# The down projection of a feed-forward block: seven block products in another order, on two chains of banks in turns, with the first unit's operands in one shared piece of SBUF

## The chip, the cores and the metric

The kernel runs on one core of one Trainium2 chip. The metric is device time in microseconds (us): the median of several executions. One more execution was recorded by the hardware profiler. TensorE multiplies matrices and writes PSUM, VectorE (DVE) and ScalarE (ACT) do element-wise work, GpSimd (POOL) does too but not on PSUM, and SyncE (SP) issues the transfers (DMA). Each engine works through its own instructions in the order in which the program lists them.

## The reference

Two layers on 1024 rows of width 1024. Each layer runs a mixer, a feed-forward block and an embedding gate:

```python
D_FF = 2816
def swiglu(h, w_gate, w_up, w_down):
    return (jax.nn.silu(h @ w_gate) * (h @ w_up)) @ w_down
...
        h = h + swiglu(rmsnorm(h, norm_ffn_g[i]), ffn_w_gate[i], ffn_w_up[i], ffn_w_down[i])
        e = rmsnorm(p[i] @ ple_w_proj[i], ple_post_norm_g[i])
        h = h + e * jax.nn.sigmoid(rmsnorm(h, ple_norm_g[i]) @ ple_w_gate[i])
```

What is changed is the last product of `swiglu`, a [1024 x 2816] by [2816 x 1024] matrix product (called "down" below, once in each layer), and the last line, the embedding gate (`ple`).

## The kernel before

**How a product is kept exact.** Operands are split in a high part that TensorE takes as fp32r and a low part that is the rest. A product is three matmuls: high by high, high by low, low by high. ACT makes the high part (a cast), DVE the low part (a subtraction).

**The seven block products.** The product is cut in 2 x 2 blocks and done with seven block products in place of eight. The left factor's seven combinations are made in the gate/up stage before (`ffn_gu`) and written to device memory (`gfD`): three of them as they are, four as sums that POOL makes in `wino` (`Sg`). The right factor has eight: four blocks of the weights as loaded (`wr_dn`, index 0 to 3) and four sums that POOL makes (`T_dn`, index 4 to 7). A line of `steps` (L965) names: the left combination, the right one, the chain of banks (a or b), whether the banks start anew, and the quarter of the result `h` (row parity, column half) to which the banks are read out after this step. Chain a starts once in a unit and chain b twice. A chain that does not start anew goes on adding to what its banks hold, after they have been read out.

**Units and steps.** The 11 pairs of weight rows go in units of 2, 3, 3 and 3 pairs (L967). A unit runs the seven steps, so there are 28 steps in a down stage. A step multiplies, for each of four row pieces (`tp`), the unit's 2 or 3 pairs with three matmuls each: 24 matmuls in the first unit, 36 in the others, 924 in a down stage. After each row piece its bank is read out into `h`, by ACT the first time that a quarter is written (L1025) and by DVE with an addition afterwards (L1023).

**What a step needs first.** The left operand is loaded into a slot (L1004); ACT casts it (`y`, L1009), DVE subtracts (`x`, L1010); ACT and DVE split the right operand into `wh` and `wl` (L1012, in the helper L108 and L109). A slot holds x, y, wh and wl for up to three pairs (24 KB of each partition). There are four such slots, s0, s1, s2 and the one of `mk(7)`, which the steps take in turn, and one special place for step 3 of the first unit. A slot is free again when the matmuls of its step are done. In the first unit a slot of 24 KB holds 16 KB of operands.

**Order of the work.** The order of each engine's instructions is fixed when the program is built: a planner simulates the run with a cost model and takes, at each engine, the ready instruction that comes first in the program's order. `high_priority` moves a piece to an earlier place in that order; `after` (`issue_after`) only puts instructions behind a named one on the same engine. Pools that follow one another share memory, so a tile of the down stage waits until the tiles of the gate/up stage under it are done with.

**After the last unit.** `ple` normalises each of the eight row tiles (`norm`, L1115: ACT squares, POOL takes the root, DVE scales, TensorE transposes into PSUM, ACT and DVE split), even tiles first, and then runs two halves of gate products (`gate`, L1118) with weights that `weights` (L1102) casts on ACT and subtracts on POOL (L1110, L1111). The norms of the even tiles are placed just before the last step of the last unit (`self.even`, L995). At most two scaled rows (`hn`) exist at a time.

Of the kernel before, what the change touches and what calls it, by code (L numbers as in the profile page):

```python
# [9 lines left out]
F32 = mybir.dt.float32  # L10
F32R = mybir.dt.float32r
# [4 lines left out]
ALU = mybir.AluOpType  # L16
# [4 lines left out]
P = 128  # L21
# [42 lines left out]
class _K:  # L64
# [879 lines left out]
    def ffn_down(self, es, l, gD):  # L944
        nc, A = self.nc, self.A
        v, gp = nc.vector, nc.gpsimd
        h = self.h
        self.psum(es, f"ffpd{l}", a=4, b=4)
        mk = lambda i: self.pool(es, f"ffn{l}d{i}")
        if l:  # L950
            rw, ta, tb, s0 = mk(2), mk(1), mk(5), mk(0)
        else:
            s0, ta, rw, tb = mk(0), mk(1), mk(2), mk(5)
        s1 = mk(3)
        s2 = mk(4)
        self.pad(es, 1, f"ffp2{l}")
        tc_ = mk(6)
        sp = [s0, s1, s2, mk(7)]
        self.pad(es, 2, f"ffp3{l}")
        s3 = mk(8)  # L960
        slots = itertools.chain(sp[:3], itertools.cycle((s0, s1, sp[3], s2)))
        raws = itertools.cycle(((self.W, "wr", 2), (self.W, "wr", 2), (rw, "dr", 3), (rw, "dr", 3), (rw, "dr", 3)))
        sums = itertools.cycle(((tc_, "T", 2), (tc_, "T", 2), (ta, "T", 1), (tb, "T", 1)))

        steps = ((0, 0, "a", True, (0, 0)), (1, 2, "b", True, (0, 0)), (3, 4, "b", True, (1, 1)), (4, 5, "a", False, (0, 1)),  # L965
                 (6, 3, "b", False, (0, 1)), (5, 6, "a", False, (1, 1)), (2, 7, "a", False, (1, 0)))
        units = ((0, 1), (2, 3, 4), (5, 6, 7), (8, 9, 10))  # L967
        seen = set()
        rest = iter(range(NT))
        raw_of = {}  # L970

        def load(p):
            home, tag, bufs = next(raws)
            raw_of[p] = home.tile([P, 2048], F32, tag=tag, bufs=bufs, name=f"wr_dn{l}_{p}")
            nc.sync.dma_start(raw_of[p], A[f"w_dn{l}"][p])

        for p in units[0]:
            load(p)
        for ui, pairs in enumerate(units):
            m = len(pairs)  # L980
            ws = []
            for p in pairs:
                raw = raw_of.pop(p)
                q = raw.rearrange("p (q n) -> p q n", q=4)
                home, tag, bufs = next(sums)
                T = home.tile([P, 4, 512], F32, tag=tag, bufs=bufs, name=f"T_dn{l}_{p}")
                self.wino(gp, [T[:, i] for i in range(4)], [q[:, i] for i in range(4)], "right")
                ws.append([q[:, i] for i in range(4)] + [T[:, i] for i in range(4)])
            banks = {}
            if not ui:  # L990
                for tp in range(4):
                    banks["b", tp] = self.tp(f"pdb{l}_0_1_{tp}", "b")
            for si, (gi, wi, chain, first, (hr, hc)) in enumerate(steps):
                if si == len(steps) - 1:
                    self.even = self.tc.cur_priority  # L995
                nm = f"{l}_{ui}_{si}"
                if (ui, si) == (0, 3):
                    x, y = [self.np.tile([P, D], F32R, tag="hn", bufs=2, name=f"sl{f}{nm}").rearrange("p (j n) -> p j n", j=2) for f in "xy"]
                    slot = s3.tile([P, 2, 2, 512], F32R, name=f"slw{nm}")
                    wh, wl = slot[:, 0], slot[:, 1]  # L1000
                else:
                    slot = next(slots).tile([P, 4, 3, 512], F32R, tag="slot", bufs=1, name=f"sl{nm}")
                    x, y, wh, wl = [slot[:, i, :m] for i in range(4)]
                nc.sync.dma_start(x.bitcast(F32), gD[pairs[0]:pairs[-1] + 1, :, gi, :].rearrange("j p n -> p j n"))  # L1004
                if si == 3 and ui + 1 < len(units):
                    for p in units[ui + 1]:
                        load(p)
                with self.after([self.last_sum] if ui == 0 and si else None):
                    nc.scalar.copy(y, x.bitcast(F32))  # L1009
                    v.tensor_tensor(x, x.bitcast(F32), y.bitcast(F32), op=ALU.subtract)  # L1010
                    for i in range(m):
                        self.split(wh[:, i], wl[:, i], ws[i][wi])  # L1012
                for tp in range(4):
                    if first and (ui or chain == "a"):
                        banks[chain, tp] = self.tp(f"pd{chain}{nm}_{tp}", chain)
                    ps = banks[chain, tp]
                    c = slice(tp * P, (tp + 1) * P)
                    for i in range(m):
                        for k, (a, b) in enumerate(((y, wh), (y, wl), (x, wh))):
                            nc.tensor.matmul(ps, a[:, i, c], b[:, i, :], start=first and i == 0 and k == 0, stop=i == m - 1 and k == 2, skip_group_check=True)  # L1020
                    hv = h[:, 2 * tp + hr, hc * 512:(hc + 1) * 512]
                    if (hr, hc) in seen:
                        v.tensor_tensor(hv, ps, hv, op=ALU.add)  # L1023
                    else:
                        nc.scalar.copy(hv, ps)  # L1025
                seen.add((hr, hc))
                t = next(rest, None) if 7 * ui + si in range(9, 25, 2) else None
                if t is not None:
                    x = self.np.tile([P, D], F32, tag="hn", bufs=2, name=f"hres{l}_{t}")
                    nc.sync.dma_start(x, self.hB[t * P:(t + 1) * P, :])  # L1030
                    gp.tensor_tensor(h[:, t, :], h[:, t, :], x, op=ALU.add)
# [50 lines left out]
    def ple(self, l, out):  # L1082
        nc, A = self.nc, self.A
        v, gp = nc.vector, nc.gpsimd
        h = self.h
        order = (0, 2, 4, 6, 1, 3, 5, 7)
        with ExitStack() as es:
            mk = lambda nm: self.pool(es, f"ple{l}{nm}")
            x = lambda nm: mk(nm).tile([P, KC, 512], F32R, name=f"{nm}_p{l}")
# [3 lines left out]
            hT = [hh, hl]  # L1093
            w1 = [mk("w1a"), mk("w1b")]
            fp = mk("e")
            self.pad(es, 9, f"plp0{l}")
            w0 = mk("w0")
            gB = self.bcast_row(self.np2, A[f"g_pn{l}"], D, "gB", f"gB_pn{l}")
            self.psum(es, f"plps{l}", tp=8)
            self.ttags = itertools.cycle(["tp"])  # L1100

            def weights(u):  # L1102
                w = []
                for kh in range(2):
                    raw = self.W.tile([P, 2048], F32, tag="wr", bufs=2, name=f"wr_pg{l}_{u}{kh}")
                    nc.sync.dma_start(raw, A[f"w_pg{l}"][u, kh])
                    wt = [(w1[kh] if u else w0).tile([P, 4, 512], F32R, name=f"w{f}_pg{l}_{u}{kh}") for f in "hl"]
                    for i in range(0, 4, 2):
                        r = raw.rearrange("p (k n) -> p k n", k=4)[:, i:i + 2]
                        nc.scalar.copy(wt[0][:, i:i + 2], r)  # L1110
                        gp.tensor_tensor(wt[1][:, i:i + 2], r, wt[0][:, i:i + 2].bitcast(F32), op=ALU.subtract)  # L1111
                    w.append(wt)
                return w

            def norm(t):  # L1115
                self.norm_T(self.np2, h[:, t, :], gB, hT, t, f"p{l}", hnp=self.np)

            def gate(u, t, w):  # L1118
                cs = slice(u * 512, (u + 1) * 512)
# [14 lines left out]
                nc.sync.dma_start(out[rows, cs], h[:, t, cs])  # L1134

            w = weights(0)
            with self.tc.high_priority(self.tc.cur_priority - self.even):
                for t in order[:4]:
                    norm(t)
            for t in order[:4]:  # L1140
                gate(0, t, w)
                norm(t + 1)
            for t in order[4:]:
                gate(0, t, w)
            w = weights(1)
            for t in order:
                gate(1, t, w)
        self.dump(f"h_ple{l}", h)
# [605 lines left out]
```

## Time and profile before

| | us |
|---|---|
| median of 3 runs (2988.99 to 2994.79) | 2994.49 |
| profiled execution, its own time | 2983.25 |
| its span, first to last instruction | 2981.5 |
| TensorE busy in the span | 2868.9 (96%) |
| DVE busy | 1871.5 (63%) |
| ACT busy | 1256.5 (42%) |
| POOL busy | 1062.8 (36%) |
| down stage of layer 0, first matmul to first transpose of the gate | 1126.53 to 1355.58 |
| down stage of layer 1 | 2652.43 to 2878.28 |

TensorE is busy nearly all the time, so what can be gained without fewer matmuls lies in the stretches in which it stands still or runs at a lower granted clock. A row of a timeline gives the start, the duration, the engine, the line, the operation, output and input by the program's names, and how many like it follow one another. In brackets stands how long the engine was idle just before, and which instruction ended that. Matmuls overlap, so a matmul's own duration (some 390 ns) is longer than the distance from one to the next.

### The profile page before, as it was taken

The numbers are of one execution on the slowest core, as the hardware profiler recorded it, in microseconds if no ns is written. First come the engines' busy times: TensorE is split into PE (matmuls) and PEld (weight loads), VectorE is DVE, ScalarE is ACT, GpSimd is POOL, SyncE is SP. The second block draws the span as 40 slices with busy tenths as digits, with TensorE's granted clock in tenths as the row PEclk, the third lists the DMA queues.
The fourth block names the chain that finished last, engine by engine and source line by source line (L and its number), as shares of the span: only waits on it lengthen the run. The fifth ranks groups of instructions, "written<-read, shape, count | busy, mean of one in ns | idle before, by whom it ended". The sixth has DMA issues, their size and how long they took to land.

```text
span 2981.5 us, 47762 instructions
## 1 busy us (share of the span) xinstructions
PE 2868.9 (96%) x19211; PEld 2387.9 (80%) x19211; DVE 1871.5 (63%) x3274; ACT 1256.5 (42%) x2226; POOL 1062.8 (36%) x931
## 2 busy tenths in 40 slices
PE   7999998999999998999999999999999999999999
PEld 7989876797888886887887777788677888877877
DVE  5799995555444448984466767664455444469871
ACT  4467725554333334334445455443233333334341
POOL 1341000114444436434213443342144444566342
PEclk9999998999999998999999999999999999999999
DMA  4122165201323225534242232223711322255422
GB/s 145 50 51 93 57 191 205 92 22 39 113 102 106 106 103 204 195 112 130 106 132 91 94 114 94 90 90 113 263 64 71 113 106 103 98 190 183 157 90 92
DMA packets 119822, 340.80 MB, mean 114 GB/s; under 512 B 11696, under 2 KB 34608, under 8 KB 101936
## 3 DMA queue, kind: packets, MB, share of 16 engines
q1 hardware_dynamic: 119600, 337.74, 32.9%
q8 instruction: 151, 2.47, 0.3%
q14 instruction: 71, 0.58, 0.1%
HBM read 240.64 MB, written 97.06 MB: 113 GB/s over the span
## 4 chain that ended last, share of the span: by engine, by line
PE 78%; DVE 10%; POOL 3%; DMA 3%; ACT 3%; issue 2%; SPq 0%; DVEq 0%; ACTq 0%; POOLq 0%
PE pga L852 16%; PE pgb L852 8%; PE pso L1361 7%; PE psp L1130 6%; PE pda L1020 6%; PE pdb L1020 4%; PE psz L216 4%; PE pgc L852 4%; PE psow L237 3%; PE psz L1621 2%; PE pskqv L227 2%; POOL T_dn L780 2%; PE y L743 2%; DVE sc L467 1%; PE pswob L237 1%
## 5 line engine op out<-in xcount | busy, mean ns | idle before, releaser
L1020 PE MATMUL pda<-sl 128*128 128x512 f32 x1008 | 236.5, 393 | 15.2 <-DVE h L1023 14.2
L1020 PEld LDWEIGHTS pda<-sl 128*128 128x128 f32 x1008 | 190.2, 189 | 57.4 <-ACT sl L108 15.5
L782 POOL TENSOR_TENSOR S<-wr_gu 128x512 f32<-128x512 f32 x44 | 67.0, 1523 | 399.9 <-DMA wr_gu<-in_w_gu_dram 392.4
L1020 PE MATMUL pdb<-sl 128*128 128x512 f32 x792 | 188.4, 395 | 3.9 <-DVE h L1023 2.5
L1020 PEld LDWEIGHTS pdb<-sl 128*128 128x128 f32 x792 | 151.0, 191 | 38.1 <-DVE h L1023 4.5
L109 DVE TENSOR_TENSOR w2l_gu<-S,w2h_gu 128x1024 fp32r<-128x1024 f32 x44 | 69.3, 1575 | 164.7 <-ACT w2h_gu L108 164.6
L1361 PE MATMUL pso<-hh,wl_od 128*128 128x512 f32 x384 | 157.1, 409 | 0.0
L1361 PE MATMUL pso<-hh,wh_od 128*128 128x512 f32 x384 | 156.9, 408 | 0.0
L1361 PE MATMUL pso<-hl,wh_od 128*128 128x512 f32 x384 | 156.5, 408 | 0.0
L1009 ACT CAST sl<-sl 128x1536 fp32r<-128x1536 f32 (+1 forms) x54 | 74.9, 1387 | 140.5 <-DMA sl<-gfD 140.5
L108 ACT CAST w2h_gu<-S 128x1024 fp32r<-128x1024 f32 x44 | 46.3, 1052 | 186.4 <-PE pga L852 94.1
L780 POOL TENSOR_TENSOR T_dn<-wr_dn 128x512 f32<-128x512 f32 x44 | 82.8, 1908 | 115.9 <-DVE sl L109 61.1
L1379 DVE SCALAR_TENSOR_TENSOR c<-pso,odcw,c 128x509 f32<-128x509 f32 (+1 forms) x144 | 107.1, 744 | 25.9 <-ACT c L1376 24.3
L1010 DVE TENSOR_TENSOR sl<-sl 128x1536 fp32r<-128x1536 f32 (+1 forms) x54 | 103.5, 1919 | 30.9 <-ACT sl L1009 30.8
L227 PE MATMUL pskqv<-wh_kqv,hh 128*128 128x256 f32 x384 | 109.4, 285 | 0.3 <-ACT wh_kqv L108 0.3
L227 PE MATMUL pskqv<-wh_kqv,hl 128*128 128x256 f32 x384 | 108.7, 283 | 0.0
L227 PE MATMUL pskqv<-wl_kqv,hh 128*128 128x256 f32 x384 | 108.3, 283 | 0.0
L603 DVE TENSOR_SCALAR_CACHE_REDUCE tk_junk<-sc,tk_f 128x1024 int8<-128x1024 f32 (+5 forms) x111 | 102.6, 924 | 1.8
L1130 PE MATMUL psp<-wh_pg,hh_p 128*128 128x512 f32 x256 | 100.5, 393 | 0.0
L153 POOL TENSOR_SCALAR nss_f<-nss_f 128x1 f32<-128x1 f32 x16 | 3.2, 198 | 272.5 <-ACT junk_f L152 272.5
L1130 PE MATMUL psp<-wh_pg,hl_p 128*128 128x512 f32 x256 | 99.7, 390 | 0.0
L1130 PE MATMUL psp<-wl_pg,hh_p 128*128 128x512 f32 x256 | 99.7, 389 | 0.0
(543 smaller groups left out, 9017.0 us busy)
## 6 DMA issues: line engine op xcount, KB each, us to landing
wr_gu<-in_w_gu_dram SPq DMA_DIRECT2D x44, 1024.0 KB
sl<-gfD SPq DMA_DIRECT2D x42, 768.0 KB
gfD<-Sg SPq DMA_DIRECT2D x22, 1024.0 KB
wr_dn<-in_w_dn_dram SPq DMA_DIRECT2D x22, 1024.0 KB
wr_od<-in_w_qkv_dram SPq DMA_DIRECT2D x12, 1024.0 KB
cD<-c SPq DMA_DIRECT2D x24, 512.0 KB
gfD<-g SPq DMA_DIRECT2D x22, 512.0 KB
wr_z<-in_w_z_dram SPq DMA_DIRECT2D x10, 1024.0 KB
```

The costliest lines, as they stand in the source:

```text
L216: nc.tensor.matmul(ps[:M, f * 512:(f + 1) * 512], a[:, kc, c], b[f][:, kc, :], start=(kc == 0 and i == 0), stop=(kc == KC - 1 and i == 2))
L227: nc.tensor.matmul(out, a[:, kc, c], b[:, kc, :], start=(kc == 0 and i == 0), stop=(kc == KC - 1 and i == 2))
L237: nc.tensor.matmul(ps[:, f * 512:(f + 1) * 512], a[:, kc, tsl], b[:, f * 512:(f + 1) * 512], start=(kc == 0 and i == 0), stop=(kc == nk - ...
L603: v.tensor_scalar(jk[:, :n], sc[b], fb, 0.0, op0=op, op1=ALU.add, accum_out=c)
L780: sub = lambda o, x, y: eng.tensor_tensor(o, x, y, op=ALU.subtract)
L852: nc.tensor.matmul(bank, a[:, kc, :], b[:, kc, :], start=first and kc == 0 and m == 0, stop=kc == 3 and m == 2, skip_group_check=True)
L1009: nc.scalar.copy(y, x.bitcast(F32))
L1010: v.tensor_tensor(x, x.bitcast(F32), y.bitcast(F32), op=ALU.subtract)
L1020: nc.tensor.matmul(ps, a[:, i, c], b[:, i, :], start=first and i == 0 and k == 0, stop=i == m - 1 and k == 2, skip_group_check=True)
L1130: nc.tensor.matmul(ps, a[:, kc, c], b, start=kc == 0 and i == 0, stop=kc == KC - 1 and i == 2)
L1361: nc.tensor.matmul(ps[:, f * 512:(f + 1) * 512], a[:, kc, :], b[f][:, kc, :], start=(kc == 0 and i == 0), stop=(kc == KC - 1 and i == 2))
L1379: nc.vector.scalar_tensor_tensor(c[:, e:(f + 1) * 512], ps[:, e - d:(f + 1) * 512 - d], cw[:, k:k + 1], c[:, e:(f + 1) * 512], op0=ALU.mul ...
```

## The change

Four things are changed, all in `ffn_down` and `ple`:

- The order of the steps: (4, 5) comes before (3, 4) and (5, 6) before (6, 3), so that the chains run a b a b a b a in place of a b b a b a a. In units 1 and 3 the two chains change places, so that a unit begins on the chain that the unit before did not end on.
- The slots: s1 and s2 become one tile `sl12` of 48 KB. The first unit takes three thirds of it (16 KB each, offsets 0, 2, 4), the later units two halves (0 and 3). With s0, `mk(7)` and the special place, the first unit's steps 0 to 4 have five places that none of them shares. In the last unit `mk(7)` is not used, so three slots go round.
- The homes of the raw weights and of the sums of the last unit: pair 10 is loaded into the `dr` buffers in place of the `wr` ones; pairs 9 and 10 take `ta` and `tb`.
- `ple`: its first weights lie 8 KB further up (pad 17 for 9), and the casts of its second weights come behind the last early norm on ACT.

```diff
-        s1 = mk(3)
-        s2 = mk(4)
+        s12 = mk(3).tile([P, 6 * 2048], F32R, name=f"sl12_{l}")
...
-        sp = [s0, s1, s2, mk(7)]
+        s7 = mk(7)
...
-        slots = itertools.chain(sp[:3], itertools.cycle((s0, s1, sp[3], s2)))
-        raws = itertools.cycle(((self.W, "wr", 2), (self.W, "wr", 2), (rw, "dr", 3), (rw, "dr", 3), (rw, "dr", 3)))
-        sums = itertools.cycle(((tc_, "T", 2), (tc_, "T", 2), (ta, "T", 1), (tb, "T", 1)))
-
-        steps = ((0, 0, "a", True, (0, 0)), (1, 2, "b", True, (0, 0)), (3, 4, "b", True, (1, 1)), (4, 5, "a", False, (0, 1)),
-                 (6, 3, "b", False, (0, 1)), (5, 6, "a", False, (1, 1)), (2, 7, "a", False, (1, 0)))
+
+        slots = itertools.chain((s0, 0, 2, None, 4, s0, 0), (s7, 3, s0, 0) * 3 + (s7, 3), (s0, 0, 3, s0, 0, 3, 0))
+        ra, rb = (self.W, "wr", 2), (rw, "dr", 3)
+        raws = iter((ra, ra, rb, rb, rb, ra, ra, rb, rb, rb, rb))
+        sums = itertools.chain(((tc_, "T", 2), (tc_, "T", 2), (ta, "T", 1), (tb, "T", 1)) * 2, ((tc_, "T", 2), (ta, "T", 1), (tb, "T", 1)))
+
+        steps = ((0, 0, "a", True, (0, 0)), (1, 2, "b", True, (0, 0)), (4, 5, "a", False, (0, 1)), (3, 4, "b", True, (1, 1)),
+                 (5, 6, "a", False, (1, 1)), (6, 3, "b", False, (0, 1)), (2, 7, "a", False, (1, 0)))
...
-                if (ui, si) == (0, 3):
+                chain = "ab"[(chain == "b") ^ (ui % 2)]
+                slot = next(slots)
+                if slot is None:
...
-                    slot = next(slots).tile([P, 4, 3, 512], F32R, tag="slot", bufs=1, name=f"sl{nm}")
-                    x, y, wh, wl = [slot[:, i, :m] for i in range(4)]
+                    if isinstance(slot, int):
+                        slot = s12[:, slot * 2048:][:, :m * 2048]
+                    else:
+                        slot = slot.tile([P, 6144], F32R, tag="slot", bufs=1, name=f"sl{nm}")[:, :m * 2048]
+                    slot = slot.rearrange("p (i j n) -> p i j n", i=4, j=m)
+                    x, y, wh, wl = [slot[:, i] for i in range(4)]
...
-            self.pad(es, 9, f"plp0{l}")
+            self.pad(es, 17, f"plp0{l}")
...
-            def weights(u):
+            def weights(u, marks=None):
...
+                    with self.after(marks):
+                        for i in range(0, 4, 2):
...
             for t in order[:4]:
                 gate(0, t, w)
-                norm(t + 1)
+                marks = norm(t + 1)
             for t in order[4:]:
                 gate(0, t, w)
-            w = weights(1)
+            w = weights(1, marks[:1])
```

## Rows read from the trace of the kernel before

**Rows 1.** Stretches of layer 0's down stage: busy us (and instructions) of each engine
```profile
1126.00:1187.00 61.00, 50.07 (x191) 38.87 (x190) 52.37 (x46) 25.81 (x42) 46.36 (x27) 0.86 0.51 185
1187.00:1323.00 136.00, 135.09 (x596) 111.32 (x595) 120.82 (x135) 53.09 (x69) 57.99 (x27) 1.00 0.50 168
```
**Rows 2.** Timeline of TensorE in layer 0's down stage
```profile
1126.53 5.65 PE L1020 MATMUL pda<-sl 128*128 128x512 f32 x24
...
1137.71 1.66 PE L1020 MATMUL pdb<-sl 128*128 128x512 f32 x6 [1.46 <-DVE g L937]
...
1142.67 0.79 PE L1020 MATMUL pda<-slw,sly 128*128 128x512 f32 x1 [3.06 <-DVE slw L109]
...
1175.48 2.90 PE L1020 MATMUL pda<-sl 128*128 128x512 f32 x6 [5.73 <-DVE h L1023]
...
1232.87 16.60 PE L1020 MATMUL pda<-sl 128*128 128x512 f32 x72 [0.91 <-DVE h L1023]
...
1339.26 16.48 PE L1020 MATMUL pda<-sl 128*128 128x512 f32 x72
1355.58 1.91 PE L193 MATMUL tp_p<-cf,hn_p 128*128 128x128 f32 x16
```
**Rows 3.** Timeline of TensorE in layer 1's down stage and behind it
```profile
2652.43 1.09 PE L1020 MATMUL pda<-sl 128*128 128x512 f32 x4
...
2697.93 2.90 PE L1020 MATMUL pda<-sl 128*128 128x512 f32 x6 [6.42 <-DVE h L1023]
...
2755.26 12.52 PE L1020 MATMUL pda<-sl 128*128 128x512 f32 x54 [0.90 <-DVE h L1023]
...
2878.28 1.91 PE L193 MATMUL tp_p<-cf,hn_p 128*128 128x128 f32 x16
...
2884.51 1.09 PE L193 MATMUL tp_p<-cf,hn_p 128*128 128x128 f32 x8 [2.66 <-DVE hn_p L203]
```
**Rows 4.** Short stretches; the third number from the right is the granted clock
```profile
1147.00:1151.50 4.50, 4.50 (x11) 3.44 (x11) 4.50 (x6) 0.59 (x1) 4.50 (x4) 0.50 0.91 337
...
2666.00:2669.00 3.00, 1.76 (x6) 0.81 (x6) 3.00 (x2) 1.10 (x2) 3.00 (x3) 1.00 0.03 13
```
**Rows 5.** Timeline of DVE in layer 0, before the longest wait
```profile
1157.62 1.64 DVE L1010 TENSOR_TENSOR sl<-sl 128x1024 fp32r<-128x1024 f32 x1 [3.10 <-ACT sl L1009]
1159.18 1.88 DVE L109 TENSOR_TENSOR sl<-wr_dn,sl 128x512 fp32r<-128x512 f32 x3
1162.60 1.29 DVE L109 TENSOR_TENSOR sl<-T_dn,sl 128x512 fp32r<-128x512 f32 x2 [1.54 <-ACT sl L108]
...
1165.55 4.61 DVE L1010 TENSOR_TENSOR sl<-sl 128x1536 fp32r<-128x1536 f32 x2 [0.46 <-ACT sl L1009]
...
1171.28 3.45 DVE L109 TENSOR_TENSOR sl<-wr_dn,sl 128x512 fp32r<-128x512 f32 x2
1174.66 0.68 DVE L1023 TENSOR_TENSOR h<-pda,h 128x512 f32<-128x512 f32 x1
```
**Rows 6.** Queue of SP: issues of the left operands, in both layers
```profile
1139.78 0.41 SPq L1004 DMA_DIRECT2D sl<-gfD  x1
...
2845.83 0.36 SPq L1004 DMA_DIRECT2D sl<-gfD  x1
```
**Rows 7.** Timeline of POOL in layer 0: the last sum of the last group
```profile
1155.64 1.28 POOL L780 TENSOR_TENSOR Sg<-g,Sg 128x512 f32<-128x512 f32 x1
```
**Rows 8.** Timeline of DVE in layer 1: opening, last unit, gate
```profile
2679.55 1.65 DVE L1010 TENSOR_TENSOR sl<-sl 128x1024 fp32r<-128x1024 f32 x1 [1.82 <-ACT sl L1009]
...
2697.11 0.68 DVE L1023 TENSOR_TENSOR h<-pda,h 128x512 f32<-128x512 f32 x1
...
2851.71 1.75 DVE L1010 TENSOR_TENSOR sl<-sl 128x1536 fp32r<-128x1536 f32 x1
...
2881.81 2.64 DVE L203 SCALAR_TENSOR_TENSOR hn_p<-h,ss_p,gB_pn 128x1024 f32<-128x1024 f32 x1
```
**Rows 9.** Timeline of ACT in layer 1's last unit: a cast behind its load
```profile
2850.10 1.48 ACT L1009 CAST sl<-sl 128x1536 fp32r<-128x1536 f32 x1 [2.59 <-DMA sl<-gfD]
```

More of the change, by code (lines that the diff above doesn't have):

```diff
@@ L1107, in weights @@
                     wt = [(w1[kh] if u else w0).tile([P, 4, 512], F32R, name=f"w{f}_pg{l}_{u}{kh}") for f in "hl"]
[L1108 to L1111, printed above, removed]
+                    with self.after(marks):
+                        for i in range(0, 4, 2):
+                            r = raw.rearrange("p (k n) -> p k n", k=4)[:, i:i + 2]
+                            nc.scalar.copy(wt[0][:, i:i + 2], r)
+                            gp.tensor_tensor(wt[1][:, i:i + 2], r, wt[0][:, i:i + 2].bitcast(F32), op=ALU.subtract)
                     w.append(wt)
@@ L1115, in norm @@
             def norm(t):
-                self.norm_T(self.np2, h[:, t, :], gB, hT, t, f"p{l}", hnp=self.np)
+                return self.norm_T(self.np2, h[:, t, :], gB, hT, t, f"p{l}", hnp=self.np)
             def gate(u, t, w):
```

## The prediction, made before the changed kernel was run

> **What bounds the kernel now.** I read the table of stretches first, to find where TensorE is not fed; then TensorE's timeline for each place where it stood still and who ended that; then the timelines of DVE, SP, ACT and POOL just before the longest wait. In the first stretch of layer 0's down stage TensorE is busy 50.07 of 61 us while DVE is busy 52.37; in the next it is busy 135.09 of 136 [rows 1]. So only the opening of a down stage (its first unit) leaves room, and in it TensorE waits for DVE.
>
> How much room: 72 matmuls take from 1339.26 to 1355.58, 0.2267 us each at full clock, so 924 take 209.5 us. The stage of layer 0 lasts 1355.58 - 1126.53 = 229.1 us [rows 2], that of layer 1 2878.28 - 2652.43 = 225.9 us [rows 3]. They lose 19.6 and 16.4 us. A wait of 0.9 us in each comes later, at a seam between units (1232.87; 2755.26); the openings lose the rest, **18.7 and 15.5 us**.
>
> The largest single wait is 5.73 us (6.42 in layer 1) before the first unit's last step, and DVE's read-out `h<-pda` ended it [rows 2, 3]. The last two steps both add to chain a, so step 6 must wait until DVE has read out step 5. DVE came to that read-out at 1174.66, behind two subtractions of 4.61 us together, one of them the second unit's, and two splits of 3.45 us that are the second unit's too [rows 5]. This is an order of work, not a lack of data. The other waits are 1.46 us (a bank still read by the gate/up stage's last product) and 3.06 us (DVE's split for the fourth step) [rows 2]. A wait can cost more than itself: behind the 3.06 us the granted clock was 0.50, the lower of the two levels (1.2 GHz), and 11 matmuls took 4.50 us; after waits of less than a microsecond it stayed at 1.00 [rows 4].
>
> **The change, part by part.**
>
> *Order of the steps and chains in turns.* No instruction is added or removed. In the first unit step 5 on b now stands between the two steps on a, so the read-out of step 4 has 24 matmuls (24 x 0.2267 = 5.4 us) more. The same holds at the seams: the next unit begins on the other chain, and the 0.91 and 0.90 us should go: **-1.8 us**. Between nothing and this I take all, since a full step of slack is nine times the wait.
>
> *Places for the first unit's operands.* Before, step 4 took s0 and so its load could not be issued until step 0 was through; SP issued it at 1139.78, after the write of the last gate values in its queue [rows 6]. DVE then ran dry three times before the long wait: 3.10 us (the cast waits for its load), 1.54 and 0.46 us, 5.1 us in all [rows 5]. Now the first five steps have places of their own; later loads come one step earlier against the matmuls that need them. By the order of the pools, `sl12` lies on tiles of the gate/up stage of which B21's high part was under s1 and its low part under s2; each B21 product reads both, so joining the two adds no wait.
>
> What is late next is DVE itself. It must have done, before the second unit begins, all the first unit's work. Before, it was there at 1174.66 + 0.68 = 1175.34. Without its 5.1 us of idling, without the second unit's split of 3.45 us that was put ahead [rows 5], and with four read-outs of about 0.65 us more that were still to come (2.6), that is 1175.34 - 5.1 - 3.45 + 2.6 = 1169.4. TensorE, with no wait, would finish the first unit's 168 matmuls at 1126.53 + 38.1 = 1164.6. So at best 4.8 us are lost in place of 18.7. The order is the planner's, not the chip's, and one such split ahead of its turn costs 3.45; I allow one: 8.3 us lost, a gain of **-10.4 us**, between 0 (DVE takes as long as before) and -18.7 (no wait at all).
>
> In layer 1 the same reckoning starts at 2697.11 + 0.68 = 2697.8, with 1.82 us of DVE's idling [rows 8]: 2697.8 - 1.8 - 3.45 + 2.6 = 2695.1 against 2652.43 + 38.1 = 2690.5, so 4.6 lost, 8.1 with one split ahead, a gain of 15.5 - 8.1 = **-7.4 us**, between 0 and -15.5. Waits this short should leave the clock up (rows 4 show it at 1.00 behind such waits), so I add nothing for it.
>
> One new dependence: the second unit's first operands move to the place of `mk(7)`, which lies on the buffer of the last `Sg` sums. POOL finished these at 1155.64 + 1.28 = 1156.9 [rows 7]; their write out and the load behind it fit before 1169, but with little to spare.
>
> *Three slots in the last unit.* Step 6 now takes the half that step 4 used, with only step 5 between them. Turnaround: issue at 2845.83, cast begins at 2850.10 and takes 1.48, subtraction ends at 2851.71 + 1.75 = 2853.46 [rows 6, 8, 9], 7.6 us against a step of 36 x 0.2267 = 8.16 us. It fits by half a microsecond if neither the casts nor the subtraction queue behind anything; on DVE, read-outs and the first norm's scaling now come in the same step. Bounds 0 and +4 us in each layer (the subtraction with POOL beside it, plus a read-out and a scaling ahead); I take **+1 us** in each, +2.0, nearest to the row.
>
> *Homes of raws and sums, pad.* Pair 10's raw weights wait for pair 7's, pairs 9 and 10's sums for pairs 6 and 7's; before, they waited for tiles of the same unit. I cost these at nothing: whole steps cover them. The gate's first weights no longer wait for the last slot, which hid behind matmuls before.
>
> *Gate.* Even rows are complete one step later (after step 5), 8.16 us before the end in place of 16.3. Two of the four norms were scaled before the end and the others waited for row buffers until the transposes, which came behind all matmuls; the last wait was 2.66 us [rows 3], and in it DVE's scaling took 2.64 us beside POOL's subtraction of the second weights [rows 8]. That subtraction now comes later. And since the last unit's chains change places, the banks that the first transposes use are those of step 5, free one step before the end, so that transposes can run inside step 6 and release the row buffers. I take 2.5 us in each layer, **-5.0 us**, between 0 and -5.3; nearer the full wait because two separate parts act on it.
>
> Sum: -1.8 - 10.4 - 7.4 + 2.0 - 5.0 = -22.6 us. Against the profiled execution's own 2983.25 us that is 2960.7; the runs shown have a median of 2994.49, 11.2 above the profiled one, and the same difference gives **2972 us**, with its own range 2961 to 2983.
>
> **A rule against it.** DVE's splits took 1.72 us each beside POOL (two in 3.45) and 0.65 without (two in 1.29) [rows 5], while its read-outs from PSUM, with one operand in SBUF, took 0.68 in either case. By this, the opening is DVE's work and POOL's work one after the other: 46.36 us of POOL in the 61 [rows 1]. The Trainium skill, SBUF — State Buffer, section Who interferes with whom, says of the port pair that the two engines share that it is "an exclusive lock", and that a VectorE instruction with two SBUF inputs contends for it; the trace agrees (1.72 against 0.65). If it alone set the opening, reordering would move the waits and shorten nothing; that is rival 1.
>
> **The rivals.**
>
> 1. *The opening stays as long, the waits only move.* DVE and POOL hold each other up for the same total. For: the stretched splits; DVE busy 52.37 of 61 us. Against: 5.1 us of DVE's idling, and 3.45 us of work that was not due. Time: the seams, the last unit and the gate alone, -1.8 + 2.0 - 5.0 = -4.8, 2990 us.
>
> 2. *Nearly all waits go.* DVE's order comes out right and the loads come in time: openings -18.7 - 15.5, seams -1.8, gate -5.0, last unit 0: -41; with a bank's wait of 1.46 us in each layer, which the change doesn't touch, left: -38, 2956 us.
>
> 3. *The shared piece is treated as one* (slower). If a load into any part of `sl12` had to wait until all earlier readers of it were done, a step on it right behind another step on it would stall for the turnaround of 7.6 us: steps 2, 5 and 6 of the last unit, and steps 2, 4 and 6 of the first in part. With three full stalls in each layer, +46, no gain in the openings, and -4.8 elsewhere, the time is 3036 us. It decides as soon as the last unit has more than one full stall in each layer and the openings stay as they are. For: parts of this tile are now named by different cuts. Against: a slot was one tile before, too, and its parts were handled one by one: the splits of the second unit's weights (1159.18) were written before that slot's left operand was there to subtract (1165.55) [rows 5].
>
> 4. *It doesn't do what it says.* The planner may put the steps' instructions in an order that undoes the turns. This is rival 1 in time.
>
> **How the numbers follow.** Forecast 0.57; rivals 1 and 4 together 0.20; rival 2 0.12; rival 3 and other stalls of the last unit 0.11. What can be told from no change here is about 0.2%, 6 us. Forecast and rival 2 are faster; rival 1 at -4.8 falls on both sides of the bound, 0.08 faster and 0.12 the same; rival 3 is slower. So 0.77 faster, 0.12 same, 0.11 slower. The range goes from rival 2 to just past rival 1: 2956 to 2994, leaving out rival 3 and the tails.
>
> **What would show it.** Right: in the openings no wait above 2 us for a read-out on chain a, the second unit's first matmul some 38 + 8 us after the stage's first, the granted clock at 1.00 throughout, transposes inside the last step. Wrong: a wait of 4 us or more before the second unit's first step with DVE busy throughout (rival 1); waits before steps 2, 5 and 6 of the last unit that end with the subtraction (rival 3), or before step 6 alone (the turnaround); a wait for `T_dn` or `wr_dn` in the last unit (the homes).

## The result, and the profile after

The changed kernel takes 2975.06 us (median of 4 runs, 2971.74 to 2976.82) against 2992.78 for the kernel before in the same comparison: a ratio of 0.9941, 95% interval 0.9924 to 0.9958. The forecast was 2972, range 2956 to 2994. The profiled execution took 2976.15 us, its span 2974.3. One execution of a later kernel ("T0, T1 first on POOL" in the table below), its profiled one, took 5288.97 us at a mean granted clock of 0.847; it is left out, so that this kernel has six runs and no timeline.

The stage of layer 0 now lasts from 1130.50 to 1353.79, 223.29 us (229.05 before), that of layer 1 from 2650.03 to 2872.50, 222.47 (225.85 before). First the table of stretches, each stage cut at the second unit's first matmul; columns as in [rows 1] (the busy times of PE, PEld, DVE, ACT and POOL, then the granted clock):

```profile
1130.50:1181.50 51.00, 42.34 (x169) 33.35 (x168) 47.54 (x39) 23.80 (x39) 48.00 (x26) 0.87 0.60 218
1181.50:1327.00 145.50, 145.50 (x643) 120.54 (x642) 128.65 (x145) 55.83 (x70) 56.63 (x28) 1.00 0.45 157
2650.03:2699.95 49.92, 42.02 (x169) 32.99 (x168) 47.69 (x38) 26.65 (x41) 48.02 (x27) 0.90 0.66 244
2699.95:2846.00 146.05, 146.05 (x644) 120.72 (x645) 128.53 (x145) 55.30 (x70) 56.62 (x28) 1.00 0.46 157
```

Behind the opening TensorE is now busy without a gap up to the last step of the last unit: the seams' 0.91 and 0.90 us are gone. In the openings DVE and POOL are both busy for 47 to 48 of 50 to 51 us. TensorE's timeline, layer 0 and then layer 1, answers to [rows 2, 3] (the matmuls are L1027 now, the read-outs L1030, the left operand's cast and subtraction L1016 and L1017):

```profile
1130.50 5.63 PE L1027 MATMUL pda<-sl 128*128 128x512 f32 x24
...
1143.89 2.93 PE L1027 MATMUL pdb<-sl 128*128 128x512 f32 x6 [3.68 <-DVE g L937]
1146.61 0.63 PE L1027 MATMUL pda<-sl 128*128 128x512 f32 x1
1152.18 7.54 PE L1027 MATMUL pda<-sl 128*128 128x512 f32 x23 [4.94 <-DVE sl L109]
...
1181.51 3.79 PE L1027 MATMUL pdb<-sl 128*128 128x512 f32 x16
...
1347.31 6.64 PE L1027 MATMUL pdb<-sl 128*128 128x512 f32 x28 [0.63 <-DVE sl L1017]
...
2652.19 4.81 PE L1027 MATMUL pda<-sl 128*128 128x512 f32 x20 [1.06 <-DVE sl L109]
...
2669.00 8.53 PE L1027 MATMUL pda<-sl 128*128 128x512 f32 x23 [6.33 <-DVE sl L109]
...
2699.95 2.30 PE L1027 MATMUL pdb<-sl 128*128 128x512 f32 x9 [0.48 <-DVE h L1030]
...
2872.50 1.91 PE L193 MATMUL tp_p<-cf,hn_p 128*128 128x128 f32 x16
...
2877.36 1.09 PE L193 MATMUL tp_p<-cf,hn_p 128*128 128x128 f32 x8 [1.30 <-DVE hn_p L203]
```

The 5.73 and 6.42 us before the first unit's last step are gone. In their place one wait of 4.94 (6.33) us stands earlier, before step 2, which DVE's split of a sum ends; in layer 0 there is also 3.68 us for the bank that the last gate product holds. Behind both the clock is at its lower level (compare [rows 4]):

```profile
1143.90:1146.60 2.70, 2.70 (x6) 2.14 (x7) 2.70 (x2) 0.00 (x0) 2.70 (x3) 0.50 0.00 0
1152.20:1156.00 3.80, 3.77 (x8) 2.56 (x9) 3.80 (x3) 2.65 (x4) 3.80 (x3) 0.50 0.00 0
...
2669.00:2673.00 4.00, 3.97 (x9) 2.67 (x10) 4.00 (x4) 1.20 (x2) 4.00 (x3) 0.50 0.00 0
```

DVE's timeline shows what stood ahead of the 4.94 us (compare [rows 5]):

```profile
1139.25 1.77 DVE L109 TENSOR_TENSOR slw<-T_dn,slw 128x512 fp32r<-128x512 f32 x1
1140.94 2.29 DVE L1017 TENSOR_TENSOR sl<-sl 128x1024 fp32r<-128x1024 f32 x1
1143.15 0.68 DVE L937 TENSOR_TENSOR g<-pga,g 128x512 f32<-128x512 f32 x1
1143.76 1.15 DVE L109 TENSOR_TENSOR sl<-T_dn,sl 128x512 fp32r<-128x512 f32 x1
1144.83 2.29 DVE L935 TENSOR_TENSOR g<-u,g 128x1024 f32<-128x1024 f32 x1
1147.05 1.75 DVE L109 TENSOR_TENSOR slw<-T_dn,slw 128x512 fp32r<-128x512 f32 x1
1148.71 5.09 DVE L109 TENSOR_TENSOR sl<-T_dn,sl 128x512 fp32r<-128x512 f32 x3
```

In these rows DVE is never idle. Splits for step 3 (`slw`) came before those of step 2, and the last gate product L937, whose matmuls had ended before 1130.50, waited behind preparations until 1143.15. Two readings are possible: a bad order on DVE, or more work for DVE and POOL than the opening has room for.

### The profile page after: what moved, and what is told of

Same layout as the page of the kernel before. It is cut to its first block, busy times and chain, and to the rows that moved or that the text cites. A ratio compares the mean times of both kernels' runs of the same rounds, so it can differ in the third digit from the quotient of the medians.

```text
span 2974.3 us, 47842 instructions
## 1 busy us (share of the span) xinstructions
PE 2867.7 (96%) x19211; PEld 2388.5 (80%) x19211; DVE 1867.2 (63%) x3274; ACT 1259.4 (42%) x2226; POOL 1060.5 (36%) x931
## 4 chain that ended last, share of the span: by engine, by line
PE 83%; DVE 8%; DMA 3%; ACT 3%; issue 2%; POOL 1%; SPq 0%; DVEq 0%; ACTq 0%; POOLq 0%
PE pga L852 16%; PE pgb L852 8%; PE pso L1369 7%; PE pdb L1027 6%; PE pda L1027 6%; PE psp L1138 6%; PE psz L216 4%; PE pgc L852 4%; PE pskqv L227 3%; PE psow L237 3%; PE psz L1629 2%; PE y L743 2%; PE pswob L237 2%; DVE sc L467 1%; PE tpp L734 1%
## 5 line engine op out<-in xcount | busy, mean ns | idle before, releaser
L1027 PE MATMUL pda<-sl 128*128 128x512 f32 x912 | 217.5, 396 | 12.4 <-DVE sl L109 12.3
L1027 PEld LDWEIGHTS pda<-sl 128*128 128x128 f32 x912 | 173.9, 191 | 51.7 <-DVE sl L109 15.4
L1027 PE MATMUL pdb<-sl 128*128 128x512 f32 x888 | 207.9, 391 | 5.4 <-DVE g L937 3.7
L1027 PEld LDWEIGHTS pdb<-sl 128*128 128x128 f32 x888 | 167.1, 189 | 41.9 <-DVE g L937 4.1
L1016 ACT CAST sl<-sl 128x1536 fp32r<-128x1536 f32 (+1 forms) x54 | 74.8, 1386 | 145.8 <-DMA sl<-gfD 143.1
L108 ACT CAST w2h_gu<-S 128x1024 fp32r<-128x1024 f32 x44 | 46.3, 1052 | 186.1 <-PE pga L852 94.1
L1017 DVE TENSOR_TENSOR sl<-sl 128x1536 fp32r<-128x1536 f32 (+1 forms) x54 | 103.3, 1914 | 24.7 <-ACT sl L1016 24.5
L600 ACT ACTIVATE tk_junka<-sc,tk_f 128x512 int8<-128x512 f32 (+2 forms) x93 | 83.7, 900 | 34.5 <-DVE tk_f L618 30.3
```

The lines of the kernel that those rows point to most:

```text
L600: nc.scalar.activation(jk[:, :n], sc[b], AF.Sign, bias=fb, scale=-1.0, accum_out=c)
```

## The experiments

"Stage" is the time from the stage's first matmul to the gate's first transpose, "2nd" and "2nd+1" the starts of the second unit's first and second step behind the stage's first matmul (38.1 and 46.3 without any wait), for layer 0 / layer 1; cells are blank where the matmuls of two units interleave or where there is no timeline. Each median is of 5 to 12 runs. The kernel before had a median of 2990.95 (29 runs) beside the first four rows of the table, 2990.91 (16) beside "casts not moved" and the three orders of DVE's and POOL's work, and 2989.63 (17) beside the other four. The ratio is the estimate on record, which differs from the quotient of the two medians by up to 0.0006.

| kernel | median us | ratio, 95% interval | stage | 2nd | 2nd+1 |
|---|---|---|---|---|---|
| the change, again | 2975.57 | 0.9944 (0.9930-0.9958) | 223.3 / 222.6 | 51.0 / 50.1 | 59.2 / 58.5 |
| order alone | 2991.37 | 1.0005 (0.9995-1.0015) | 226.9 / 223.9 | | |
| places alone | 2998.81 | 1.0027 (1.0018-1.0036) | 229.3 / 228.8 | | |
| casts alone | 2988.40 | 0.9988 (0.9979-0.9997) | 228.9 / 227.7 | | |
| change, casts not moved | 2984.26 | 0.9977 (0.9965-0.9989) | 223.1 / 222.6 | 50.8 / 50.1 | 59.0 / 58.5 |
| change, no exchange of chains | 2981.83 | 0.9972 (0.9963-0.9982) | 227.3 / 225.9 | | |
| step 2 first on DVE | 2979.99 | 0.9959 (0.9946-0.9972) | 225.4 / 222.7 | 53.1 / 50.4 | 61.3 / 58.6 |
| T0, T1 first on POOL | 2978.40 | 0.9952 (0.9939-0.9966) | | | |
| both | 2983.03 | 0.9971 (0.9961-0.9981) | 225.4 / 224.5 | 53.2 / 49.1 | 61.3 / 60.5 |
| second unit's sums late | 2977.63 | 0.9960 (0.9948-0.9973) | 226.0 / 221.9 | 49.1 / 49.6 | 61.9 / 57.8 |
| sums late, step 2 first | 2977.82 | 0.9964 (0.9951-0.9978) | 222.9 / 223.0 | 45.5 / 45.4 | 58.8 / 58.8 |
| sums late, gate product first | 2976.33 | 0.9954 (0.9941-0.9968) | 223.1 / 225.0 | 49.5 / 51.9 | 58.9 / 60.9 |

### The parts by themselves

The change once more, run beside its parts. Expected:

> The changed kernel once more, for a tighter ratio and a second trace. In its first trace the down stages lasted 223.3 and 222.5 us (before 229.1 and 225.9) and the last wait ahead of the gate 1.30 us (before 2.66), together -11.9 us, while the medians differ by 17.7 (interval 12.6 to 22.7). Theory: the change is worth what these stretches show, 12 us, ratio 0.996. Rival: there is a gain outside of them, and the ratio stays at 0.994.

It repeats to 0.5 us in the median, and the stages to 0.2. The next three kernels are the kernel before with one part each: the order with the exchange of chains; the places of slots, raws and sums with the gate's pad; the later casts.

```diff
# order alone
+        steps = ((0, 0, "a", ...), (1, 2, "b", ...), (4, 5, "a", ...), (3, 4, "b", ...), (5, 6, "a", ...), (6, 3, "b", ...), (2, 7, "a", ...))
+                chain = "ab"[(chain == "b") ^ (ui % 2)]
# places alone
+        s12 = mk(3).tile([P, 6 * 2048], F32R, name=f"sl12_{l}")
+        slots = itertools.chain((s0, 0, 2, None, 4, s0, 0), (s7, 3, s0, 0) * 3 + (s7, 3), (s0, 0, 3, s0, 0, 3, 0))
+            self.pad(es, 17, f"plp0{l}")
# casts alone
+                    with self.after(marks):
+            w = weights(1, marks[:1])
```

> Only the order of the steps and the chains' turns; slots, homes of raws and sums, pad and the gate's casts as before. Theory (the turns of the chains are the gain): the waits of 5.73 and 6.42 us for a read-out on chain a go, the seams' 0.9 too, the stages come to 223 to 225 us in each layer, the total falls by 7 to 10 us. Rival (the places for the first unit's operands are the gain): DVE still runs dry before step 4's load, the stages stay within 2 us of 229 and 226, the total within 4 us.

> Only the homes: the shared piece, the slots, the raws, the sums and the pad as in the changed kernel; order of steps, chains and the gate's casts as before. Theory (turns): the wait for the read-out before the first unit's last step stays at 5 us or more in both layers, the stages stay within 2 us of 229 and 226. Rival (places): DVE doesn't run dry any more, the stages fall to 223 to 225.

> Only the gate's second weights behind the last early norm on ACT; everything else as before. Theory: the last wait ahead of the gate falls from 2.66 to 1.30 us in both layers, since the scaling no longer runs beside POOL's subtraction; the stages don't change; total -2.7 us. Rival (the transposes inside the last step, by the chains' turns, were what shortened this wait): it stays at 2.66, total unchanged.

Order alone 1.0005, no difference; places alone slower by 7.9 us; casts alone faster by 2.6. By themselves the three add up to 5.7 us slower, together they are 15.4 faster: they work only together. The openings are one place where they hinder each other. TensorE's timeline with the order alone and, below, with the places alone, in layer 0:

```profile
1179.79 4.18 PE L1021 MATMUL pdb<-sl 128*128 128x512 f32 x9 [5.96 <-DVE h L1024]
```
```profile
1148.03 2.93 PE L1026 MATMUL pdb<-sl 128*128 128x512 f32 x6 [6.12 <-DVE g L937]
```

With the order alone the old 5.73 us move to the second unit's start, on chain b, still behind DVE's work. With the places alone the first steps' operands arrive early, DVE prepares them early, and the last gate product stands behind them: 6.12 us.

The other place is the gate. With the order alone the two stages together are 4.2 us shorter, but the gate's transposes wait 1.64 and 2.99 us in each layer (0.56 and 2.67 before), 2.8 us more in all. With the places alone the stages are 3.2 us longer, and the transposes wait 2.21 and 2.97 us behind the 0.56, 5.0 us more than before. The later of these waits, in layer 0 with the order alone and in layer 1 with the places alone:

```profile
1367.07 1.97 PE L193 MATMUL tp_p<-cf,hn_p 128*128 128x128 f32 x8 [2.99 <-DVE hn_p L203]
```
```profile
2908.57 1.94 PE L193 MATMUL tp_p<-cf,hn_p 128*128 128x128 f32 x8 [2.98 <-DVE hn_p L203]
```

In both kernels POOL's subtractions of the gate's second weights stand where DVE scales, which the moved casts take away: 1.30 us is left in the change. The order with the moved casts, and the places with them, were not run.

### The casts and the exchange of chains, taken out of the change

```diff
-            w = weights(1, marks[:1])
+            w = weights(1)
```

> The changed kernel, but the casts of the gate's second weights are not put behind the last early norm. With the order of steps alone the median was 2991.4, with the places alone 2998.8, with the casts alone 2988.4, and with all three 2975. Theory A (order and places work together, each alone only moves the opening's wait; the casts are worth the gate's 1.4 us in each layer and its clock): the stages stay at 223 and 222.5 us, a wait of 2.6 to 3.0 us returns at the gate with some matmuls at half clock behind it, 2979 to 2984. Theory B (the casts' place is what the openings' gain hangs on, by the planner's order): the stages go back to 226 to 229 us, 2990 or more.

The stages stay (theory A), and the median is 8.7 us above the change's, most of it lost at the gate. POOL's and then TensorE's timeline of this kernel in layer 1:

```profile
2873.70 11.03 POOL L1119 TENSOR_TENSOR wl_pg<-wr_pg,wh_pg 128x1024 fp32r<-128x1024 f32 x4
2884.82 0.46 POOL L153 TENSOR_SCALAR ss_p<-ss_p 128x1 f32<-128x1 f32 x2
```
```profile
2877.81 1.09 PE L193 MATMUL tp_p<-cf,hn_p 128*128 128x128 f32 x8 [2.21 <-DVE hn_p L203]
...
2887.37 1.07 PE L193 MATMUL tp_p<-cf,hn_p 128*128 128x128 f32 x8 [2.99 <-DVE hn_p L203]
```

The second weights' subtractions, 11.03 us in one piece, slow DVE's scaling and hold the next norm's root back to 2884.82. The waits at the gate are 2.21 and 2.99 us in place of 1.30 in layer 1, and 2.21 and 1.36 in layer 0: 6.2 of the 8.7 us (2.27 + 3.90); the rest is not located. In the old order the moved casts are worth 2.6 us in all (casts alone), with the new order and places 8.7.

```diff
-                chain = "ab"[(chain == "b") ^ (ui % 2)]
```

> The changed kernel, but each unit starts on chain a (a b a b a b a): the two chains do not change places in units 1 and 3. If the turns of the chains are what took the seam's wait away: a wait of 0.5 to 1 us at the start of a unit returns in each layer, +1 to +2 us against the change, 2976 to 2977. If the order within the unit took it away: no wait at the seams, 2975. If the second unit's start on the bank that the first unit's last step used is what binds: a wait of 3 to 6 us before it, 2982 to 2987.

The seam's wait is back, as the first theory had it (though with 0.5 to 1 us), 1.43 us in layer 0 and 1.45 in layer 1, but the price is higher than that: the stages are 4.0 and 3.4 us longer, the median 6.3 above the change's. TensorE's timeline, layer 0:

```profile
1248.87 4.38 PE L1026 MATMUL pda<-sl 128*128 128x512 f32 x18 [1.43 <-DVE h L1029]
```

Some 2 us more are lost in the second unit, which could not start on chain a behind step 6 on a, and began with a piece of its second step.

### An order of DVE's work, or too much work?

Three kernels put the work in the order in which TensorE needs it: on ACT and DVE the first unit's steps 3 to 6 behind step 2's splits; on POOL the sums T0 and T1 of both pairs ahead of T2 and T3; both.

```diff
+                with self.after(([self.last_sum] + (held if si > 2 else [])) if ui == 0 and si else None):
...
+                if (ui, si) == (0, 2):
+                    held = list(marks)
```

> The changed kernel, but in the first unit the casts, subtractions and splits of steps 3 to 6 stand, on ACT and DVE, behind the splits of step 2 (its right operands are sums). Theory A (the 3.68 us and the 4.94 and 6.33 us waits that the change left are an order of DVE's work: the splits of steps 3 and 4 stand ahead of step 2's, and the last gate product behind them): the long wait before step 2 falls below 2 us, the 3.68 us goes, the granted clock stays near 1.00, the second unit begins 43 to 46 us after the stage's first matmul in place of 51.0 and 49.9, the stages last 216 to 219 us in place of 223.3 and 222.5; about -8 us against the change, 2967. Theory B (the sums that step 2 needs come late from POOL, which makes T0 and T2 of a pair before T1): the 3.68 us goes, the wait before step 2 stays at 3 us or more, stages 221 to 223. Theory C (DVE's and POOL's total work bounds the opening): the waits move to later steps, the second unit still begins 50 to 51 us after the first matmul, 2975.

> The changed kernel, but POOL makes, in the first unit, the two sums that steps 2 and 6 come first to (T0, T1) of both pairs before it makes the other two (T2, T3) of either. Theory A (DVE's order alone): nothing changes, the waits of 3.68, 4.94 and 6.33 us stay within 0.5 us, 2975. Theory B (POOL's sums come late): the wait before step 2 falls from 4.94 and 6.33 to below 2 us, about -6 us against the change, 2969. Theory C (total work of DVE and POOL): no change, the second unit begins 50 to 51 us after the first matmul.

> Both edits: on DVE and ACT the first unit's steps 3 to 6 behind the splits of step 2, and on POOL the sums T0, T1 of both pairs before T2, T3. Theory A: as with the first edit alone, stages 216 to 219 us, 2967. Theory B: only both together take the wait before step 2 below 1 us, stages 215 to 218, 2965, at least 3 us less than with the first edit alone. Theory C: the second unit begins 50 to 51 us after the first matmul as in the change, 2975.

None is faster than the change: the medians are 2.8 to 7.5 us above it, where theories A and B had 6 to 10 us less for some of them, so both fall. Theory C, with the second unit's start at 50 to 51 us, comes nearest (49.1 to 53.2), but had the time as in the change. With the first, TensorE's timeline in layer 0 is:

```profile
1141.16 5.76 PE L1030 MATMUL pda<-sl 128*128 128x512 f32 x24 [1.86 <-ACT h L1035]
1152.31 1.22 PE L1030 MATMUL pdb<-slw,sly 128*128 128x512 f32 x2 [5.40 <-DVE h L1033]
...
1174.18 7.35 PE L1030 MATMUL pda<-sl 128*128 128x512 f32 x24 [2.34 <-DVE h L1033]
```

Step 2 starts 12.9 us after the stage's first matmul, where the change had all but one of its matmuls stand until 21.7, and all of it is given back: step 3 waits 5.40 us for a read-out that stands in DVE's queue behind the splits that were put back, and step 6 waits again. With both edits it is one wait of 8.58 us at the same place.

The read-out for which step 6 waits is late for another reason as well. SP's, ACT's and then DVE's timeline of the first kernel:

```profile
1155.51 0.39 SPq L1012 DMA_DIRECT2D sl<-gfD  x1
```
```profile
1164.10 1.05 ACT L1017 CAST sl<-sl 128x1024 fp32r<-128x1024 f32 x1 [14.27 <-DMA sl<-gfD]
```
```profile
1165.18 1.57 DVE L1018 TENSOR_TENSOR sl<-sl 128x1024 fp32r<-128x1024 f32 x1 [4.42 <-ACT sl L1017]
```

DVE is idle for 4.42 us, for the left operand of step 6. Its place was free when step 1 had ended, at 1139.3, but SP issued the load at 1155.51, behind two loads of weights whose buffers DVE's splits had still to free.

### Taking POOL's work out of the opening

If DVE and POOL hold each other up, DVE must get faster where POOL has less to do. The second unit's sums get the places that the first unit's leave, so POOL cannot make them before the first unit's last splits:

```diff
-        sums = itertools.chain(((tc_, "T", 2), (tc_, "T", 2), (ta, "T", 1), (tb, "T", 1)) * 2, ...
+        sums = iter(((tc_, "T", 2),) * 4 + ((ta, "T", 1), (tb, "T", 1), (tc_, "T", 2), (tc_, "T", 2), (ta, "T", 1), (tb, "T", 1), (tc_, "T", 2)))
```

> The changed kernel, but the sums of the second unit are given the places that the first unit's sums leave, so that POOL can make them only when the first unit's last splits are through; DVE's order in the opening stays as in the change up to the resumption at 1152 us. Theory L (DVE's and POOL's two-operand work hold each other up, so that the opening lasts as long as both together): without POOL's some 8 sums (1.7 us each) between 1140 and 1160 DVE's splits there take 0.65 to 1.2 us in place of 1.7, the wait before step 2 falls from 4.94 and 6.33 us to 1 to 3, the second unit begins 46 to 48 us after the stage's first matmul in place of 51.0 and 49.9, the stages last 218 to 220 us; about -7 us against the change, 2968. Theory D (DVE's own work, or the casts and loads, bound the opening whatever POOL does): waits and stages within 0.7 us of the change's, 2975. Theory S (the late sums are missed): a wait for sums of the second unit before its step 2, 2980 or more.

POOL's timeline of this kernel, and then DVE's, in layer 0:

```profile
1132.98 7.88 POOL L780 TENSOR_TENSOR T_dn<-wr_dn,T_dn 128x512 f32<-128x512 f32 x4
1144.36 1.65 POOL L782 TENSOR_TENSOR Sg<-g 128x512 f32<-128x512 f32 x1 [3.50 <-DVE g L935]
```
```profile
1142.47 0.68 DVE L109 TENSOR_TENSOR sl<-T_dn,sl 128x512 fp32r<-128x512 f32 x1
1143.07 1.21 DVE L935 TENSOR_TENSOR g<-u,g 128x1024 f32<-128x1024 f32 x1
1144.20 0.68 DVE L109 TENSOR_TENSOR slw<-T_dn,slw 128x512 fp32r<-128x512 f32 x1
1144.81 5.10 DVE L109 TENSOR_TENSOR sl<-T_dn,sl 128x512 fp32r<-128x512 f32 x3
```

DVE's instructions are in the same order as in the change's timeline above. While POOL is idle a split takes 0.68 us (1.15 and 1.75 there) and L935 1.21 (2.29); when POOL works again at 1144.36, three splits take 5.10, 1.70 each. So it is shown instruction by instruction that POOL's work stretches DVE's, and in layer 0 the wait before step 2 falls from 4.94 to 2.33 us as theory L said. In layer 1 the first unit's own sums and those of the gate values filled POOL's time there all the same, and the wait stayed (6.30). But the time did not fall: what POOL does not do early it does late. That is clearest with the late sums and step 2 first together:

> The late sums of the second unit together with the other order on DVE and ACT (the first unit's steps 3 to 6 behind the splits of step 2), which alone moved the waits to the read-outs of steps 3 and 6 (5.40 and 2.34 us) and left the stages at 225.4 and 222.7. Theory L: the read-out that steps 3 waits for comes 3 to 5 us earlier, stages 217 to 220 us, 2968 to 2972. Theory D: 225 and 222.5 us as with the order alone, 2980.

The second unit begins 45.5 us after the stage's first matmul, what the prediction had asked for. Then TensorE's timeline shows a new wait, and DVE's its cause:

```profile
1176.95 4.37 PE L1034 MATMUL pdb<-sl 128*128 128x512 f32 x18
1184.39 5.97 PE L1034 MATMUL pdb<-sl 128*128 128x512 f32 x18 [3.07 <-DVE h L1037]
```
```profile
1182.64 1.09 DVE L109 TENSOR_TENSOR sl<-T_dn,sl 128x512 fp32r<-128x512 f32 x1 [3.71 <-ACT sl L108]
1183.66 1.27 DVE L1037 TENSOR_TENSOR h<-pdb,h 128x512 f32<-128x512 f32 x2
```

A split of a late sum stands at the head of DVE's queue, idle for 3.71 us, and the read-outs that TensorE needs stand behind it. The second step begins at 58.8 us, as in the change.

> The late sums of the second unit, and the last product of the gate values, whose bank the second step waits for (3.68 us in layer 0), ahead of the first unit's preparations from step 2 on. Theory L: the 3.68 us falls below 1, the wait before step 2 to 1 to 3 us, stages 216 to 219 us, 2965. Theory D: the 3.68 us is added to the wait before step 2, stages as in the change, 223 and 222.5.

Putting the last gate product first, too, takes away the 3.68 us, and step 2 then waits 8.68 in one piece, as theory D said: 3.68 + 4.94 = 8.62 before.

What follows: five kernels moved the waits over different steps, and the second unit's second step began 57.8 to 61.9 us after the stage's first matmul in all of them (59.2 and 58.4 in the change). The stretch up to there, of layer 0, in the change and, below, with the late sums and step 2 first (columns as above):

```profile
1130.50:1189.67 59.17, 50.51 (x206) 40.11 (x204) 55.71 (x50) 28.05 (x44) 48.00 (x26) 0.88 0.56 201
```
```profile
1131.44:1190.20 58.76, 50.60 (x206) 40.30 (x205) 51.04 (x48) 28.13 (x46) 47.38 (x26) 0.94 0.55 201
```

In the change DVE is busy for nearly all of it, and the two engines hold each other up. With the late sums DVE is idle for 7.7 us, and the step begins only 0.4 us earlier: the read-outs that TensorE needs stand behind a sum that comes late. So the sum of DVE's and POOL's work does not explain every run: a late sum or a late load in front of a queue held some of them back. What bounds the change itself is not settled, since a kernel with part of the sums left out, or with the load of step 6 issued earlier, was not run.

## Why the prediction was right or wrong

The time was right, within 3.1 us, in part by luck, as the last paragraph of this section shows; the account behind it was not right in all its terms. Of the four signs that it named for being right, one held: no wait above 2 us for a read-out on chain a in the openings. The second unit began 51.0 and 49.9 us after the stage's first matmul in place of 46, the clock fell, and no transpose ran inside the last step. By the prediction's own steps:

| step | forecast us | measured us |
|---|---|---|
| openings, layer 0 / layer 1 | -10.4 / -7.4 | -5.8 / -3.7 |
| seams | -1.8 | -1.8 |
| three slots in the last unit | +2.0 | +1.3 |
| gate | -5.0 | -2.7 |
| sum | -22.6 | -12.7 |

**Openings: the step "8.3 us lost" failed.** The loss was 51.0 - 38.1 = 12.9 us in layer 0 and 49.9 - 38.1 = 11.8 in layer 1. Two things were mis-sized. The clock was said to stay at 1.00; behind the waits it was 0.50, and 6 and 23 matmuls took 2.72 and 7.38 us in place of 1.36 and 5.2 (3.5 us), in layer 1 23 took 8.36 (3.1 us). Without that 9.4 and 8.7 us would be lost, close to the 8.3 and 8.1 forecast, but by luck: the forecast had the loss at the second unit's start, and it came at steps 1 and 2. And the waits were not short: the new step 2 needs sums, DVE split them last, and I had not followed the operands of the step that moved forward. DVE's end was worked out for the whole unit, by taking its 5.1 us of idling out of the old timeline. In the change, in layer 0, DVE was not idle up to the splits of step 2, which is where TensorE stood, and POOL stretched many of its instructions there; its idle 3.46 us came later, where no matmul waited for it. The Trainium skill, SBUF — State Buffer, section Who interferes with whom, says that a VectorE instruction with two SBUF inputs contends with a GpSimd one that reads SBUF; 0.68 against 1.70 us agrees. So rival 1 was wrong on the time, since the openings did get shorter, but its mechanism is at work in what is left, if not alone (see the experiments). Rival 2 (nearly all waits go) and rival 4 (the turns are undone) are out by the same timeline: two long waits remain in layer 0 and one in layer 1, and none is for a read-out on chain a. (Rival 2 counted a bank's wait of 1.46 us in each layer that the change would not touch: in layer 1 no matmul waited for the last gate product before, and in layer 0 that wait grew to 3.68.)

**Seams: right in size, too small in weight.** The 0.91 and 0.90 us went. Taking the exchange of chains out again costs 4.0 and 3.4 us of stage, because in the new order each unit would begin on the chain that has just ended.

**Three slots: right.** Only step 6 of the last unit waits, 0.63 and 0.62 us, and as the bound had it: the subtraction took long beside POOL and its cast stood behind others. ACT's and DVE's timeline in layer 1 (compare [rows 8, 9]):

```profile
2856.03 3.90 ACT L1118 CAST wh_pg<-wr_pg 128x1024 fp32r<-128x1024 f32 x4
...
2860.87 1.47 ACT L1016 CAST sl<-sl 128x1536 fp32r<-128x1536 f32 x1
```
```profile
2862.37 3.59 DVE L1017 TENSOR_TENSOR sl<-sl 128x1536 fp32r<-128x1536 f32 x1
...
2876.03 1.27 DVE L203 SCALAR_TENSOR_TENSOR hn_p<-h,ss_p,gB_pn 128x1024 f32<-128x1024 f32 x1
```

There is no wait before steps 2 and 5, so rival 3 (the shared piece treated as one) is out, and none for raws or sums: costing the homes at nothing held in the last unit.

**Gate: half of it.** The scaling that ended the last wait took 1.27 us (last line above) in place of 2.64, since POOL's subtraction had moved: 1.37 us a layer, also with the casts alone. The second part, transposes inside the last step, did not happen: the 16 transposes still come at 2872.50, after all matmuls, with the same 0.56 us behind them. Free banks did not make the planned order use them.

**Why the time came out all the same.** The terms that the trace shows come to -12.7 us; taken directly, the two stages and the last wait at each gate are 11.9 us shorter. The medians differ by 15.4 (2990.95 to 2975.57), so about 3 us are not located. The two profiled executions differ by 7.1 (2983.25 to 2976.15): the kernel before was profiled in an execution shorter than any of its later 29, and 4.0 us of that stand in the stretch before the down stage of layer 0, where nothing is changed, which lasts 1126.53 us there and 1130.50 after. And the three runs that the forecast started from had a median 3.5 us above the later 29. From those, a gain of 22.6 would have given 2968: the gain was forecast some 7 us too large, and the high start hid half of it.

## What to carry to other kernels

When a step is moved forward, follow each of its operands back through every engine's queue to the data, not only the bank that it freed. Where DVE and POOL are both busy for nearly the whole of a stretch with two-operand work, don't count idle time taken from one of them as gained: here every reordering only moved the wait. Look for work that can leave the stretch altogether, and for loads that stand behind others in SP's queue. Parts that each gain little or lose can be worth 15 us together, so test a part by taking it out of the whole as well as by putting it in alone.

## What the runs showed of the hardware that was not expected

The length of a wait does not say by itself whether the clock falls. Both kernels' TensorE had run at full clock before the wait; behind 1.86 us (step 2 first on DVE) the clock stayed at 1.00, behind 1.80 us (both edits) it was 0.56 in the next 3.8 us, and 24 matmuls took 7.2 us in place of 5.4:

```profile
1141.20:1146.60 5.40, 5.40 (x24) 4.38 (x24) 5.40 (x4) 3.87 (x7) 5.40 (x4) 1.00 0.02 6
```
```profile
1175.70:1179.50 3.80, 3.80 (x10) 2.98 (x11) 3.80 (x5) 3.17 (x5) 0.47 (x1) 0.56 0.52 193
```

The first line is of the former kernel, the second of the latter.
